# Fewer plain tiles between the staged part and the pair tiles of a feed-forward block, with the operand sums begun a stage earlier

## The chip, the cores and the metric

The kernel runs on one core of a Trainium2 chip. Its inputs are in device memory, and everything that the reference computes, from the modulation vectors to the final norm, is done in one launch. The metric is the device time of one execution in microseconds, as the median of several runs; smaller is better. All arithmetic stands for 32-bit floats: a product is made as three matmuls of split operands (see below), so that its error stays near that of float32.

## The reference

One layer over 256 latent tokens `x` and 256 context tokens `ctx` of width 2048. The change concerns the first half of it only, the two feed-forward products with the same weights for both streams:

```python
h  = h  + 0.5 * mod[:, 2] * swiglu(modulate(h,  norm_ffn1[l], mod[:, 0], mod[:, 1]), w_ffn1_in[l], w_ffn1_out[l])
hc = hc + 0.5 * mc[2]     * swiglu(modulate(hc, norm_ffn1[l], mc[0],     mc[1]),     w_ffn1_in[l], w_ffn1_out[l])

def swiglu(h, w_in, w_out):
    gate, up = jnp.split(h @ w_in, 2, axis=-1)
    return (jax.nn.silu(gate) * up) @ w_out
```

`w_ffn1_in` is 2048 x 11264 (5632 gate columns, 5632 up columns), `w_ffn1_out` 5632 x 2048. Latents and context stand side by side as 512 columns: the first 256 (`:T`) are latents, the others (`T:`) context. Behind it come a mixer (gated linear attention and a convolution), a second feed-forward block for the latents, and a norm; the change does not touch them.

## The kernel before, in words

**Three matmuls for one.** Each operand is split into a high part (rounded to the fast 32-bit matmul type) and a low part (the rest). `split` writes hi with a cast on ACT and lo with a subtraction on DVE; a weight half of 128x1024 becomes `whi` and `wlo` in the same way. A product is then hi·whi + lo·whi + hi·wlo, three matmuls on PE. Every one of those rows is recorded at the helper's line L64, so tiles are told apart by name. Weight halves pass through three buffers (`NW = 3`), raw weights through four (`NRAW = 4`).

**The 44 tiles of hidden columns** (f = 0 to 43, 128 gate and 128 up columns each) are made in three ways.

1. *Tiles 0 to 7, staged over K.* The inner dimension of 2048 is 16 slices of 128 (kt), and `STAGES = [1, 1, 1, 1, 2, 2, 4, 4]` runs over them as they become ready. The last stage holds kt 12 to 15: eight half steps of 24 matmuls of 128x512. Its `evac` adds each product to `part` on DVE; every second one also runs Silu on ACT, a product on DVE, a split into hi and lo, and `keep_hid`, which stores the two to memory by two DMAs that POOL issues (L954).
2. *Plain tiles, f = 8, 9, 10* (`NSTD = 3`, loop `for f in range(NFT0, FT)`, `ffn_tile`): four half steps of 24 matmuls of 128x512 each, 96 in all.
3. *Pair tiles, f = 11 to 43* (`pair_tile`, L866): gate and up, and both token streams, are combined so that seven block products take the place of eight. A block product is 24 matmuls of 128x256, so a pair tile has 168. The seven are, in this order, "11", p, s2, "12", s3, q, "22". Some need sums of weight blocks (`make_t1`, `factor`; the up block is added by an accumulating DMA that POOL issues, L184), and p, s2, s3 and q need sums of the operands.

**The sums of the operands** are made once, by `sums_x(j)` for j = 0 to 7 (L828 to L851); in the texts, sum 1 is j = 0 and sum 8 is j = 7. Each is: two adds on POOL at L831 (`xa`, `xb`: hi + lo of slices j and j + 8); two subtractions on DVE into `xm`; a split of `xm` (hi on ACT, lo on DVE), which is what the second product p and the third, s2, read for slice j; `qf` and `xn` on DVE, and the split of `xn` into `s3`. `place_q` splits `qf` later into the places of the context columns.

**What sets the order.** `after_start` (L814) is a step appended after the last stage: it starts the loads of small tables, opens the pool of the pair tiles, loads the vector `sc` for a wide job on DVE (L653) and runs Silu over it on ACT, and puts the eight `sums_x` into the deque `slow`; `set_rate(HK, 4 * NSTD - 3)` says over how many weight steps they are given out. A list scheduler of the framework then places the instructions of each engine in a queue; what is wrapped in `keep` stays in program order. At run time each queue runs strictly in its order, and semaphores make it wait.

Of the kernel before, what the change touches and what calls it, by code (L numbers as in the profile page):

```python
# [34 lines left out]
NMRAW = 4  # L35
NF2 = 4
HB = 3
NSTD = 3
HK = KT // 2
XP2 = 12  # L40

# [74 lines left out]
def layer_kernel(ctx: ExitStack, tc: tile.TileContext, A):  # L116
# [20 lines left out]
    def gt(p="g", dt=F32, shape=(128, 512), n=512):  # L137
        t = gpool.tile([128, 2 * (T + 2)], dt, tag="g", name=nm(p))[:, :n]
        return t if len(shape) == 2 else t.rearrange("p (a t) -> p a t", a=shape[1])

    def pst():
        return pspool.tile([128, 512], F32, tag="ps", name=nm("ps"))
# [27 lines left out]
    def P(fn):  # L170
        steps.append(("p", None, 0, fn))
# [175 lines left out]
    def set_rate(n, total):  # L347
        rate["credit"], rate["r"] = 0.0, n / total
# [9 lines left out]
    def mm3(ps, w, c, x, start, stop, more=False):  # L358
        hi, lo = w[0][:, c : c + 128], w[1][:, c : c + 128]
        PE.matmul(ps, hi, x[0], start=start, stop=False, skip_group_check=more)  # L360
        PE.matmul(ps, hi, x[1], start=False, stop=False, skip_group_check=more)
        PE.matmul(ps, lo, x[0], start=False, stop=stop, skip_group_check=more)
# [120 lines left out]
    def open_x():  # L483
        modscope.close()
        xbox["t"] = xscope.enter_context(tc.tile_pool(name="xpool", bufs=1))
# [15 lines left out]
    def mod_cols(k0, nk):  # L501
        F = 128 * nk
        g = 1024 // F
        st = {}

        def part(c, u):
            def f(raw):
                if c == 0 and u == 0:
                    st["ps"] = pst()
                for i in range(g):  # L510
                    kt = u * g + i
                    j = kt % 4
                    PE.matmul(
                        st["ps"][32 * j : 32 * j + 32, :F],
                        csil[c][:, kt, :],
                        raw[:, i * F : (i + 1) * F],
                        start=c == 0 and kt < 4,
                        stop=c == 1 and kt >= KT - 4,
                    )
                if c == 1 and kt == KT - 1:  # L520
                    st["msb"] = gt("msb")
                    S.copy(out=st["msb"][:, :F], in_=st["ps"][:, :F])

            return f

        mvs = []
        for c in range(2):
            for u in range(KT // g):
                n = mod_unit[0]
                src = A["wmodK"][n // 2, :, 1024 * (n % 2) : 1024 * (n % 2) + 1024]  # L530
                mvs.append(lambda src=src, fn=part(c, u): M(src, fn))
                mod_unit[0] += 1

        def fin():
            psT = pst()
            for i in range(nk):
                PE.matmul(
                    psT[:, 4 * i : 4 * i + 4], st["msb"][:, i * 128 : (i + 1) * 128], sel, start=True, stop=True
                )
            pv = psT[:, : 4 * nk].rearrange("p (k c v) -> p c k v", c=2, v=2)  # L540
            ks = slice(k0, k0 + nk)
            for v, m, a in ((0, modL, A1L), (1, modC, A1C)):
                V.tensor_tensor(out=m[:, 0:2, ks], in0=pv[:, :, :, v], in1=bmod[:, 0:2, ks], op=ALU.add)
                coef_scale(a[:, ks], m[:, 1, ks], norm(0)[:, ks])

        return mvs, fin
# [104 lines left out]
    def wide_vec(t):  # L651
        xbox["sc"] = t
        nc.sync.dma_start(out=t, in_=A["cvec"][0:1, :].broadcast_to([128, 2048]))  # L653
        keep(S.activation(t, t, AF.Silu))
# [54 lines left out]
    def gate_silu(psg, n=512):  # L709
        p = gt("p")  # L710
        S.activation(p[:, :n], psg, AF.Silu)
        return p
# [9 lines left out]
    NM0 = 2 * NFT0  # L722
# [3 lines left out]
    def prep(si):  # L726
        def f():
            for kt in range(starts[si], starts[si] + STAGES[si]):
                if kt % 2 == 0 and kt:
                    xnorm(kt // 2)  # L730
                xprep1(kt)

        return f

    P(stats1)
    P(norm1a)
    mvs, fin = mod_cols(0, STAGES[0])
# [8 lines left out]
    for si, nk in enumerate(STAGES):  # L746
        kbase = starts[si]
        last = si == len(STAGES) - 1
        per = 16 // nk

        def mstep(un, mm, si=si, nk=nk, kbase=kbase, per=per, last=last):
            m = un * per + mm

            def mm_one(whalf, ps, i, c):
                kt = kbase + i
                mm3(ps, whalf, c, (xh[kt], xl[kt]), i == 0, i == nk - 1)

            def evac(ps):
                if si == 0:
                    part[m] = gt("part")  # L760
                    S.copy(out=part[m], in_=ps)
                else:
                    V.tensor_tensor(out=part[m], in0=ps, in1=part[m], op=ALU.add)
                if last and m % 2 == 1:
                    p = gate_silu(part[m - 1])
                    return finish_keep(m // 2, p, part[m])

            return mm_one, evac

        halfsteps = []  # L770
        for u in range(NM0 // per):
            ms = [mstep(u, mm) for mm in range(per)]

            def half(hf, ms=ms, nk=nk, per=per):
                def f(hi, lo):
                    lates = []
                    for mm in range(per):
                        if mm * nk // 8 != hf:
                            continue
                        ps = pst()  # L780
                        for i in range(nk):
                            ms[mm][0]((hi, lo), ps, i, (mm * nk + i) % 8 * 128)
                        late = ms[mm][1](ps)
                        if late:
                            lates.append(late)

                    def go():
                        for x in lates:
                            x()

                    return go

                return f

            un = Unit(A["w1a"][w0], 2048)
            w0 += 1
            halfsteps += [("w", un, 0, half(0)), ("w", un, 1, half(1))]
        nh = len(halfsteps)
        before, after = [[] for _ in range(nh)], [[] for _ in range(nh)]
        if not last:  # L800
            k1 = kbase + nk
            at = max(0, nh - FINAT)
            mvs, fin = mod_cols(k1, STAGES[si + 1])
            for i, mv in enumerate(mvs):
                before[i * (at + 1) // len(mvs)].append(mv)
            after[at].append(lambda fin=fin, si=si: (P(fin), P(prep(si + 1))))
        for i in range(nh):
            for x in before[i]:
                x()
            steps.append(halfsteps[i])  # L810
            for x in after[i]:
                x()

    def after_start():  # L814
        nc.sync.dma_start(out=smx, in_=A["smallm"])
        nc.sync.dma_start(out=ctri, in_=A["ctri"])
        open_x()
        wide_vec(xbox["t"].tile([128, 2048], F32, name="sc"))
        slow.extend(lambda j=j: sums_x(j) for j in range(HK))
        set_rate(HK, 4 * NSTD - 3)  # L820

    P(after_start)

# [111 lines left out]
    def ffn_tile(wg, wu, f, get_x, fin, n, gate=None):  # L937
        box = {}

        def g(ps):  # L940
            box["p"] = gate(ps) if gate else gate_silu(ps, n)

        in_steps(wg, get_x, g, n)
        in_steps(wu, get_x, lambda ps: fin(f, box.pop("p"), ps, n), n)
# [22 lines left out]
    def finish_keep(f, p, psu, n=512):  # L967
        late = finish_ft(f, p, psu, n)

        def go():  # L970
            late()
            keep_hid(f)
            if f // CH_FT < NCH - 1:
                del hid[f]

        return go
# [58 lines left out]
    for f in range(NFT0, FT):  # L1035
        w = [A["w1b"][2 * (f - NFT0) + i] for i in range(2)]
        if f < NFT0 + NSTD:
            ffn_tile(*w, f, get1, finish_keep, 512)
        else:
            if f == NFT0 + NSTD:  # L1040
                P(flush_slow)
# [992 lines left out]
```

## Time and profile before

| what | value |
|---|---|
| median of the runs | 2707.22 us (2707.12 to 2707.38) |
| the profiled execution's own time | 2703.02 us |
| its span on the core | 2701.3 us |
| PE busy | 2654.8 us, 98% of the span, 18964 matmuls |
| DVE busy | 1878.8 us, 70% |
| ACT busy | 1123.8 us, 42% |
| POOL busy | 188.2 us, 7% |
| mean granted PE clock | 0.995 |
| first matmul of the last stage | 200.69 us |
| first matmul of the first pair tile | 312.15 us |

The shares are of the whole span. What decides about one stage is read in that stage: how many matmuls it has, how long PE stood still in it, and which engine it waited for. A timeline row gives start, duration, engine, line, operation, output tile and input tiles, the count of equal instructions that are put together, and in brackets the idle time of the engine before it with what ended it.

### The profile page before, as it was taken

The page shows a single profiled execution, that of the slowest core. Times are in us where ns is not written, and L with a number is a line of the kernel's source. Part 1 is how long each engine was busy: PE and PEld are TensorE (multiplying, and loading weights), DVE is VectorE, ACT ScalarE, POOL GpSimd, SP SyncE. Part 2 cuts the span into 40 slices and gives each one's busy share as a digit, 9 for nine tenths or more (in the row PEclk, how much of TensorE's full clock was granted, in tenths as well). Part 3 has the DMA queues.
Part 4 walks back from the last instruction along what each step waited for, and adds up shares of the span by engine and source line. Part 5 has one row for each costly group of instructions (what it writes and reads, how often), then busy time and mean ns, then how long its engine had stood idle before and what let it go on. Part 6 is the DMA issues. An engine that isn't in the chain of part 4 may idle for free.

```text
span 2701.3 us, 45665 instructions
## 1 busy us (share of the span) xinstructions
PE 2654.8 (98%) x18964; PEld 2450.7 (91%) x18964; DVE 1878.8 (70%) x2553; ACT 1123.8 (42%) x1498; POOL 188.2 (7%) x212
## 2 busy tenths in 40 slices
PE   7999999999999999999999999999999999999998
PEld 5668899999999988888888988789999999999998
DVE  6656877777777764798799988476876654454543
ACT  5234455554555531122114544254554444444443
POOL 0002311111111100001002100000100000000000
PEclk9999999999999999999999999999999999999999
DMA  9854578778788899669974534455567765555553
GB/s 373 299 183 156 146 221 256 227 235 256 220 256 228 242 326 402 238 233 368 329 247 164 172 123 157 156 184 206 174 223 276 276 228 183 186 182 188 186 186 117
DMA packets 126635, 608.33 MB, mean 225 GB/s; under 512 B 14682, under 2 KB 15066, under 8 KB 78172
## 3 DMA queue, kind: packets, MB, share of 16 engines
q1 hardware_dynamic: 109308, 546.69, 56.7%
q0 software_dynamic: 16544, 57.68, 9.8%
q8 instruction: 148, 2.42, 0.3%
q10 hardware_dynamic: 576, 1.05, 0.1%
q14 instruction: 59, 0.48, 0.0%
HBM read 580.20 MB, written 25.17 MB: 224 GB/s over the span
## 4 chain that ended last, share of the span: by engine, by line
PE 57%; issue 28%; DVE 2%; DMA 0%; ACT 0%; POOL 0%; POOLq 0%; ACTq 0%; DVEq 0%
PE ps L64 57%; DVE wlo L64 1%; DMA raw<-in_w1b 0%; DVE y L64 0%; DVE junk L64 0%; ACT whi L64 0%; DVE E L64 0%; DVE h L64 0%; DVE lo L64 0%; POOL h L1905 0%; DVE raw L64 0%; DVE xs L64 0%; POOLq L2029 0%; ACT L64 0%; DVE t L64 0%
## 5 line engine op out<-in xcount | busy, mean ns | idle before, releaser
L64 PE MATMUL ps<-hi,whi 128*128 128x256 f32 (+1 forms) x4736 | 1441.9, 307 | 9.9 <-ACT whi L64 3.9
L64 PE MATMUL ps<-lo,whi 128*128 128x256 f32 (+1 forms) x4736 | 1446.9, 306 | 0.6 <-DVE lo L64 0.6
L64 PE MATMUL ps<-hi,wlo 128*128 128x256 f32 (+1 forms) x4736 | 1438.4, 306 | 3.4 <-DVE wlo L64 3.3
L64 DVE TENSOR_TENSOR wlo<-raw,whi 128x1024 fp32r<-128x1024 f32 (+1 forms) x654 | 804.1, 1230 | 564.1 <-ACT whi L64 556.0
L64 ACT CAST whi<-raw 128x1024 fp32r<-128x1024 f32 (+1 forms) x654 | 680.1, 1040 | 1235.9 <-PE ps L64 1192.0
L64 PEld LDWEIGHTS ps<-hi,whi 128*128 128x128 f32 x4736 | 892.8, 189 | 67.4 <-issue 11.3
L64 PEld LDWEIGHTS ps<-lo,whi 128*128 128x128 f32 x4736 | 893.4, 189 | 48.5 <-issue 2.9
L64 PEld LDWEIGHTS ps<-hi,wlo 128*128 128x128 f32 x4736 | 891.1, 189 | 49.4 <-DVE wlo L64 4.0
L64 DVE CUSTOM_DVE_ANT_0 junk<-mraw,mraw 128x1024 bf16<-128x1024 f32 x192 | 238.8, 1244 | 4.9 <-DMA mraw<-in_wmodT 1.9
L64 PE MATMUL ps<-hh,wlo 128*128 128x256 f32 x704 | 198.0, 281 | 0.0
L64 PE MATMUL ps<-hh,whi 128*128 128x256 f32 x704 | 197.7, 281 | 0.0
L64 PE MATMUL ps<-hl,whi 128*128 128x256 f32 x704 | 197.4, 280 | 0.0
L64 ACT CAST whi<-t 128x1024 fp32r<-128x1024 f32 x99 | 104.0, 1050 | 148.4 <-PE ps L64 147.8
L64 DVE TENSOR_TENSOR wlo<-t,whi 128x1024 fp32r<-128x1024 f32 x99 | 121.1, 1223 | 40.2 <-ACT whi L64 40.2
L64 PEld LDWEIGHTS ps<-hl,whi 128*128 128x128 f32 x704 | 132.6, 188 | 0.0
L64 PEld LDWEIGHTS ps<-hh,whi 128*128 128x128 f32 x704 | 132.6, 188 | 0.0
L64 PEld LDWEIGHTS ps<-hh,wlo 128*128 128x128 f32 x704 | 132.5, 188 | 0.0
L64 DVE TENSOR_TENSOR part<-ps,part 128x512 f32<-128x512 f32 x112 | 72.6, 685 | 64.8 <-PE ps L64 64.5
L64 PE MATMUL ps<-s,whi 128*128 128x256 f32 x528 | 94.6, 280 | 0.0
L64 PEld LDWEIGHTS ps<-s,whi 128*128 128x128 f32 x528 | 80.5, 188 | 0.0
L64 DVE TENSOR_TENSOR t<-t,raw 128x1024 f32<-128x1024 f32 x66 | 80.4, 1219 | 0.0
L1032 POOL TENSOR_TENSOR nacc<-nacc,sq 128x512 f32<-128x512 f32 x19 | 37.3, 1979 | 572.5 <-ACT sq L64 572.3
(206 smaller groups left out, 2005.2 us busy)
## 6 DMA issues: line engine op xcount, KB each, us to landing
raw<-in_w2b SPq DMA_DIRECT2D x84, 1024.0 KB, 4.9
raw<-in_w1b SPq DMA_DIRECT2D x72, 1024.0 KB, 8.0
raw<-in_wmodT SPq DMA_DIRECT2D x64, 1024.0 KB, 6.3
mraw<-in_wmodT SPq DMA_DIRECT2D x96, 512.0 KB, 5.8
raw<-in_w1o SPq DMA_DIRECT2D x47, 1024.0 KB, 7.4
mraw<-in_wmodK SPq DMA_DIRECT2D x64, 512.0 KB, 7.6
raw<-in_w2o SPq DMA_DIRECT2D x32, 1024.0 KB, 4.9
hi<-hidd SPq DMA_DIRECT2D x80, 256.0 KB, 6.5
```

Of the source, the lines that this page charges most:

```text
L64: i = f(*a, **k)
L1032: eng.tensor_tensor(out=acc, in0=acc, in1=sq, op=ALU.add)
```

## The change

`NSTD` goes from 3 to 1: only f = 8 is a plain tile, and f = 9 to 43 are pair tiles. The body of `after_start` moves into `begin_x`, and the step that calls it is appended before the half steps of the last stage instead of after the staged part. `set_rate` gives the eight sums out over 8 + 4·1 − 2 = 10 weight steps, counted from there; it was 4·3 − 3 = 9, counted from the first plain tile.

```diff
-NSTD = 3
+NSTD = 1
...
+    def after_start():
+        begin_x()
+
...
             halfsteps += [("w", un, 0, half(0)), ("w", un, 1, half(1))]
+        if last:
+            P(after_start)
         nh = len(halfsteps)
...
-    def after_start():
+    def begin_x():
         nc.sync.dma_start(out=smx, in_=A["smallm"])
         nc.sync.dma_start(out=ctri, in_=A["ctri"])
         open_x()
         wide_vec(xbox["t"].tile([128, 2048], F32, name="sc"))
         slow.extend(lambda j=j: sums_x(j) for j in range(HK))
-        set_rate(HK, 4 * NSTD - 3)
-
-    P(after_start)
+        set_rate(HK, NM0 // 2 + 4 * NSTD - 2)
```

Lines behind the change stand three lower in the changed kernel: the adds L831 are L834 there, the stores L954 are L957.

How the queues stand before and now is shown at two places of the program, the start of the last stage and the first pair tile, at the second on three engines. A name ends in a number of its own in each kernel, and the same number in before and now does not mean the same tile.

*ACT at the start of the last stage.* whi373 is a half weight of the stage, hi363 the high part of slice 13, sc the wide vector. Before:

```order
L64 ACTIVATE xs362_1687<-h15_112,modL_79,coef_81 128x256
L64 ACTIVATE xs362_1687<-h16_114,modC_80,coef_81 128x256
L64 CAST whi373_1738<-raw324_1431 128x1024
L64 CAST hi363_1690<-xs362_1687 128x512
L64 ACTIVATE xs365_1696<-h17_116,modL_79,coef_81 128x256
```

Now:

```order
L64 ACTIVATE xs362_1687<-h15_112,modL_79,coef_81 128x256
L64 ACTIVATE xs362_1687<-h16_114,modC_80,coef_81 128x256
L64 CAST whi373_1738<-raw324_1431 128x1024
L64 ACT_TABLE_LOAD
L64 ACTIVATE sc_1748<-sc_1748 128x2048
L64 CAST hi363_1690<-xs362_1687 128x512
L64 ACTIVATE xs365_1696<-h17_116,modL_79,coef_81 128x256
```

A table load and the Silu of sc now stand ahead of hi363; before, the table load stood some rows further on, ahead of the first Silu of p, and the Silu of sc behind the stage.

*ACT around the first pair tile.* In before whi545 is the half weight of the first pair's first product and whi554 that of p; hi522, hi534 and hi550 are the high parts of sums 6, 7 and 8 (hi550 stands three rows below the last row shown, whi554 two below that). Before:

```order
L64 CAST hi522_2424<-xm521_2419 128x512
L64 CAST hi527_2462<-p503_2360 128x512
L64 CAST s3511_2377<-xn524_2429 128x256
L64 CAST whi541_2514<-raw454_2132 128x1024
L64 CAST hi534_2477<-xm533_2472 128x512
L64 CAST s3536_2481<-xn539_2485 128x256
L64 CAST whi545_2546<-raw470_2212 128x1024
L64 ACTIVATE p544_2544<-ps540_2489 128x512
L64 CAST hi62_274<-qf465_2177 128x256
L64 CAST hi96_394<-qf465_2177 128x256
L64 CAST hi135_550<-qf490_2280 128x256
L64 CAST hi166_696<-qf490_2280 128x256
```

Now, where whi520 is the half weight of p, whi531 that of block "12", hi476, hi494 and hi504 the high parts of sums 5, 6 and 7, and p465 and p484 are Silu rows of tiles of the last stage:

```order
L64 CAST whi520_2333<-t1442_2016 128x1024
L64 CAST s3433_1973<-xn453_2041 128x256
L64 CAST hi459_2080<-p456_2073 128x512
L64 ACTIVATE p465_2116<-part107_426 128x512
L64 CAST hi469_2126<-p465_2116 128x512
L64 CAST whi531_2420<-raw408_1893 128x1024
L64 CAST hi476_2141<-xm475_2136 128x512
L64 ACTIVATE p484_2181<-part111_438 128x512
L64 CAST hi201_853<-qf480_2147 128x256
L64 CAST s3478_2145<-xn481_2149 128x256
L64 CAST hi487_2188<-p484_2181 128x512
L64 CAST hi494_2203<-xm493_2198 128x512
```

In before the casts of sums 6 and 7 stand ahead of the first product's half weight and sum 8's ahead of p's; now those of sums 5 to 8 stand behind the half weights of p and of block "12", whi531, whose buffer is that of the first product's.

*POOL around the first pair tile*, from the second half of the sums on. xa and xb are the two adds of a sum, hidd the stores of hid, the rows at L184 accumulating DMAs. Before (sums 5 to 8):

```order
L831 TENSOR_TENSOR xa506_2366<-hi201_853,lo202_854 128x512
L831 TENSOR_TENSOR xb507_2367<-hi360_1683,lo361_1684 128x512
L184 DMA raw496_2318<-in_w1b 128x1024
L831 TENSOR_TENSOR xa519_2417<-hi204_860,lo205_861 128x512
L831 TENSOR_TENSOR xb520_2418<-hi363_1690,lo364_1691 128x512
L954 DMA hidd529_2466<-hi527_2462 128x512
L831 TENSOR_TENSOR xa531_2470<-hi248_1083,lo249_1084 128x512
L831 TENSOR_TENSOR xb532_2471<-hi366_1699,lo367_1700 128x512
L954 DMA hidd530_2467<-lo528_2463 128x512
L831 TENSOR_TENSOR xa547_2550<-hi251_1090,lo252_1091 128x512
L831 TENSOR_TENSOR xb548_2551<-hi369_1706,lo370_1707 128x512
```

Now (sums 5 to 8):

```order
L957 DMA hidd471_2130<-hi469_2126 128x512
L834 TENSOR_TENSOR xa473_2134<-hi201_853,lo202_854 128x512
L834 TENSOR_TENSOR xb474_2135<-hi360_1683,lo361_1684 128x512
L957 DMA hidd472_2131<-lo470_2127 128x512
L957 DMA hidd489_2192<-hi487_2188 128x512
L834 TENSOR_TENSOR xa491_2196<-hi204_860,lo205_861 128x512
L834 TENSOR_TENSOR xb492_2197<-hi363_1690,lo364_1691 128x512
L957 DMA hidd490_2193<-lo488_2189 128x512
L834 TENSOR_TENSOR xa501_2243<-hi248_1083,lo249_1084 128x512
L834 TENSOR_TENSOR xb502_2244<-hi366_1699,lo367_1700 128x512
L834 TENSOR_TENSOR xa513_2292<-hi251_1090,lo252_1091 128x512
L834 TENSOR_TENSOR xb514_2293<-hi369_1706,lo370_1707 128x512
```

Before, the sixteen stores of the last stage all stood ahead of the first add; now they stand between the adds, so that sum 6's adds stand behind a store that waits for ACT's cast hi487, and those of sums 7 and 8 behind one that waits for DVE's lo488.

*PE in the second product of the first pair*, at its slices 4 to 6 before, 5 and 6 now. ps570 is p in before, ps536 now; ps543 is block "12". Before:

```order
L64 MATMUL ps570_2688<-hi500_2327,wlo555_2592 128x256
L64 MATMUL ps570_2688<-hi509_2373,whi554_2591 128x256
L64 MATMUL ps570_2688<-lo510_2374,whi554_2591 128x256
L64 MATMUL ps570_2688<-hi509_2373,wlo555_2592 128x256
L64 MATMUL ps570_2688<-hi522_2424,whi554_2591 128x256
L64 MATMUL ps570_2688<-lo523_2425,whi554_2591 128x256
```

Now:

```order
L64 MATMUL ps543_2495<-hi369_1706,whi531_2420 128x256
L64 MATMUL ps543_2495<-lo370_1707,whi531_2420 128x256
L64 MATMUL ps543_2495<-hi369_1706,wlo532_2421 128x256
L64 MATMUL ps536_2430<-hi476_2141,whi520_2333 128x256
L64 MATMUL ps536_2430<-lo477_2142,whi520_2333 128x256
L64 MATMUL ps536_2430<-hi476_2141,wlo521_2334 128x256
L64 MATMUL ps536_2430<-hi494_2203,whi520_2333 128x256
```

The 24 matmuls of block "12", of which the last three are shown, now stand inside p, between its fourth and fifth slice; before, p's 24 stood in a row.

## Rows read from the trace of the kernel before

**Rows 1.** Utilisation by windows: length, busy time per engine, clock, DMA share, GB/s.

```profile
200.00:300.00 100.00, 99.93 (x432) 80.83 (x431) 75.69 (x92) 42.37 (x59) 29.96 (x35) 1.00 0.46 148
400.00:500.00 100.00, 100.00 (x847) 100.00 (x847) 78.16 (x86) 51.81 (x71) 15.62 (x21) 1.00 0.81 237
```

**Rows 2.** PE's timeline, last stage and first pair; idle before in brackets.

```profile
200.69 1.08 PE L64 MATMUL ps<-hi,whi 128*128 128x512 f32 x4
...
204.40 1.09 PE L64 MATMUL ps<-hi,whi 128*128 128x512 f32 x4
...
312.15 0.28 PE L64 MATMUL ps<-hi,whi 128*128 128x256 f32 x1
...
315.42 0.38 PE L64 MATMUL ps<-hi,whi 128*128 128x256 f32 x1 [0.27 <-ACT whi L64]
...
316.88 0.39 PE L64 MATMUL ps<-hi,wlo 128*128 128x256 f32 x1 [0.96 <-DVE wlo L64]
...
322.33 0.39 PE L64 MATMUL ps<-hi,whi 128*128 128x256 f32 x1 [2.58 <-ACT whi L64]
```

**Rows 3.** Utilisation by windows, last stage and plain tiles.

```profile
210.00:250.00 40.00, 39.93 (x173) 32.05 (x172) 29.45 (x40) 20.50 (x26) 8.81 (x16) 1.00 0.58 203
250.00:310.00 60.00, 60.00 (x261) 48.80 (x260) 49.41 (x55) 19.82 (x29) 24.43 (x22) 1.00 0.42 125
```

**Rows 4.** POOL's timeline in the plain tiles.

```profile
250.06 1.31 POOL L831 TENSOR_TENSOR xa<-hi,lo 128x512 f32<-128x512 f32 x1
...
276.39 1.62 POOL L831 TENSOR_TENSOR xa<-hi,lo 128x512 f32<-128x512 f32 x1
...
280.13 1.61 POOL L831 TENSOR_TENSOR xb<-hi,lo 128x512 f32<-128x512 f32 x1
...
302.06 0.59 POOL L954 DMA_DIRECT2D hidd<-lo  x1 [1.91 <-DVE s L64]
302.67 1.30 POOL L831 TENSOR_TENSOR xa<-hi,lo 128x512 f32<-128x512 f32 x1
```

**Rows 5.** DVE's timeline, plain tiles and first pair.

```profile
257.77 1.22 DVE L64 TENSOR_TENSOR wlo<-raw,whi 128x1024 fp32r<-128x1024 f32 x1 [1.59 <-ACT whi L64]
258.92 0.42 DVE L64 TENSOR_TENSOR xm<-xa,xb 128x256 f32<-128x256 f32 x1
...
275.90 6.40 DVE L64 TENSOR_TENSOR lo<-xm,hi 128x512 fp32r<-128x512 f32 x1 [0.21 <-ACT hi L64]
...
288.46 0.68 DVE L64 TENSOR_TENSOR lo<-xm,hi 128x512 fp32r<-128x512 f32 x1
...
302.47 3.84 DVE L64 TENSOR_TENSOR wlo<-raw,whi 128x1024 fp32r<-128x1024 f32 x1
...
325.09 2.28 DVE L64 CUSTOM_DVE_ANT_0 raw<-raw,sc 128x2048 f32<-128x2048 f32 x1
```

**Rows 6.** ACT's timeline, last stage and plain tiles.

```profile
201.62 0.62 ACT L64 CAST hi<-xs 128x512 fp32r<-128x512 f32 x1
...
215.66 1.28 ACT L64 ACT_TABLE_LOAD   x1
...
247.84 1.91 ACT L64 ACTIVATE sc<-sc 128x2048 f32<-128x2048 f32 x1
...
301.39 1.04 ACT L64 CAST whi<-raw 128x1024 fp32r<-128x1024 f32 x1
```

**Rows 7.** The load of sc: its issue on SP's queue, and all its landings.

```profile
188.73 0.33 SPq L653 DMA_DIRECT2D sc<-in_cvec  x1
...
DMA to landing us min/median/max: 6.1/6.1/6.1
```

**Rows 8.** Utilisation by windows, first pair and a later wait.

```profile
320.00:325.00 5.00, 2.67 (x22) 2.67 (x23) 4.55 (x4) 3.76 (x6) 1.45 (x2) 1.00 0.61 146
1470.00:1475.00 5.00, 1.93 (x15) 1.52 (x13) 5.00 (x9) 3.00 (x7) 2.18 (x1) 1.00 0.56 206
1475.00:1480.00 5.00, 5.00 (x30) 5.00 (x31) 4.32 (x5) 2.94 (x5) 2.89 (x2) 0.66 0.01 3
```

## The prediction

> **What bounds the kernel now.** I read the utilisation by windows first. From 200 to 300 us PE is busy all the time with 432 matmuls of 128x512, so one costs 100 / 432 = 0.2315 us; from 400 to 500, where the pair tiles run evenly, 847 of 128x256 fill the window, 0.118 us each [rows 1]. PE is the bound in both, at full granted clock, so a tile costs its count of matmuls, plus whatever PE waits. Next comes PE's own timeline where the change acts [rows 2]: the last stage begins at 200.69, the three plain tiles follow it without a gap, and the first pair tile begins at 312.15. There PE waits three times, 0.27 + 0.96 + 2.58 = 3.81 us, for whi and wlo, which ACT and DVE make. Third, DVE's share: 29.45 of 40 us in the last stage and 49.41 of 60 in the plain tiles [rows 3]; it has room, but no more than about a fifth in the second stretch. Fourth, the timelines of POOL and DVE [rows 4, 5]: the sixteen adds of the eight sums start at 250.06, the last two at 302.67 and 1.25 later, spread over the plain tiles, and while POOL adds, a DVE subtraction with two SBUF inputs stretches: lo<-xm, 0.68 us when free, takes 6.40 beside the four adds that begin at 276.39, and wlo, 1.22 when free, takes 3.84 at 302.47 although POOL's add is recorded 0.20 later. POOL wins, and DVE finishes when POOL stops.
>
> **Part 1, fewer plain tiles.** A plain tile is 96 matmuls, 96 x 0.2315 = 22.2 us; a pair tile is 168, 168 x 0.118 = 19.8. Two tiles change kind: 2 x (19.83 - 22.22) = **-4.8 us**. These are matmuls of the engine that bounds, so all of it is on the path.
>
> **Part 2, the wide vector's Silu comes earlier.** The order has the table load and ACT's Silu of sc ahead of the cast hi363 of the last stage, instead of behind the stage. The two take 1.28 and 1.91 us [rows 6]. In before hi363 starts at 201.62 and lasts 0.62; it would be ready at 201.6 + 3.2 + 0.6 = 205.45. PE reads it first at 204.40 [rows 2], and in the new order two matmuls stand before it that stood behind, so at 204.86: a wait of **+0.6 us**, with 0 and 1.1 as its ends. Its data are no cause: the load is issued at 188.73 and lands 6.1 later [rows 7]. The table load is the one that stood ahead of p's first Silu at 215.66, so none is added.
>
> **Part 3, the sums move into the last stage, but not all of them.** Before, the adds of sums 1 to 8 have 62 us from 250 to the first pair. Now the first add cannot be issued before the last stage has begun, in POOL's queue the adds stand between the stores of hid, each of which waits for an ACT cast or a DVE subtraction, and the order shows that only sums 1 to 4 stand ahead of ACT's cast for the first pair's second product. Sums 5 to 8 stand behind whi531, the cast that can only start when PE has finished the first product of the pair (its buffer is that of whi511). So they start when PE is already in the pair, and p, the second product, needs all eight: PE's order keeps four of its eight steps, then puts the 24 matmuls of block 12 in between, and then sums 5 to 8 one after the other.
>
> I walk this chain from t0, the end of the first product, about 270.9 (last stage to 245.8, one plain tile of 22.2 to 268.0, 24 matmuls of 0.118 to 270.9). Durations: ACT 1.05 for 128x1024 and 0.62 for 128x512, DVE 1.22, 0.68 and 0.42, a POOL add 1.25 from start to start, a store 0.6 [rows 4 to 6]. (a) whi531 0.1 to 1.15, while POOL has just taken sum 5's two adds (2.5 us) and holds DVE until 2.1: wlo532 3.3. (b) two short xm rows 4.05, hi476 4.75, ACT's Silu 5.3, DVE's lo, qf and xn rows and the product p by 6.85, hi487 7.5. (c) its store 8.2, then sum 6's two adds to 10.7; lo488 stands beside them and ends at 11.3, the store that waits for it at 12.1. (d) now sums 7 and 8 follow without a pause, four adds, 5.0 us, to 17.1: DVE's lo495 is held as in the 6.40 row and ends at 17.7. (e) five short DVE rows to 19.5, hi504 20.2, lo505 21.0, qf and xn 21.7, ACT's Silu of the plain tile and its product 22.3, t2's sum 23.5, the small rows and sum 8's xm to 24.9, ACT's whi523 and copy to 25.6, hi516 26.2, lo517 27.0. PE ends p at 27.2. Without waits the 48 matmuls of p and block 12 would end at 48 x 0.118 = 5.7. PE therefore waits 27.2 - 5.7 = **+21.5 us**. The 3.81 us of waits before [rows 2] are of the same buffers and are inside the walk, so they fall away: **-3.8**.
>
> If POOL's adds held DVE nowhere, (a), (c), (d) and the rest shrink and p would end at about 21.6, a wait of 15.9: that is the lower end. The upper end is a chain in which ACT's and DVE's rows also wait for each other once more at each sum, 4 x 1 us: 25.5.
>
> **Part 4, what follows.** DVE comes out of the chain late, and in the third and fourth product PE waits again for wlo541, which stands behind DVE's wide job of 2.28 us [rows 5], and for the copy of the first product, 0.3: **+2.6**, between 0 and 4. After a wait of PE of 2.50 + 0.56 us, in which it was busy 1.93 of 5, the granted clock of the next 5 us was 0.66 [rows 8], which is (1 - 0.66) x 5 = 1.7 us lost; after the present 2.58 it was not touched. The new waits are longer: **+1.7**, between 0 and 3. From the second pair on, ACT and DVE have their usual order, and the rest of the program differs by single places: 0.
>
> **Sum.** -4.8 - 3.8 + 0.6 + 21.5 + 2.6 + 1.7 = +17.8 us. Against the profiled execution's 2703.0 that is 2720.8; its median of the runs is 4.2 higher, 2707.2, so 2725.0.
>
> The Trainium skill, "SBUF — State Buffer", section "Who interferes with whom", says that VectorE and GpSimd exclude each other by a lock on a shared port, and whoever issued first keeps it. The rows of the 6.40 and 3.84 us agree that they exclude each other, but in the second POOL's recorded start is the later one; nothing in the sum hangs on who issued first.
>
> **Rivals.** (1) *The sums do get done in the last stage.* For it: PE keeps its 45 us there, and DVE is idle a quarter of it. Against it: the order holds half of the sums behind whi531, and all of their 16 adds would have to fit between the stores. It decides at sum 8's lo being ready by 270.9 + 5.4. Then only -4.8 - 3.8 + 0.6 = -8.0 is left: 2699. Chance 0.04. (2) *The chain is there, but DVE is not held by the adds in it.* It decides at lo495 taking 0.7 and not 5. 15.9 in place of 21.5: +12.2, 2719.4. Against it are the two stretched rows above. Chance 0.2. (3) *The waits only eat the gain:* p's wait is 5 to 10 us because sums 5 and 6 are done before t0, DVE being ahead of my walk: between 0 and +5, 2707 to 2712. Against it: hi476 stands behind whi531 on ACT, whatever DVE does. Chance 0.07. (4) *The second pair waits too,* because the sums' late tail shifts the loads and DVE's half-weights: one more wait as long as half the first, 8 to 11: +27, 2734 and more. For it: DVE needs 78.16 of 100 us in even pairs [rows 1], so a backlog of 5 us takes over 20 us to clear; against it: ps2, s3 and q are needed once, and the raw buffers are loaded long before. Chance 0.13. My forecast, slower by 17.8, is on the slower side, and rival (1) is the one on the other.
>
> **How the numbers follow.** Forecast 0.56, rivals 0.04, 0.2, 0.07 and 0.13. The range takes the forecast with the ends of its terms (15.9 to 25.5 for the wait, 0 to 4 for the tail, 0 to 3 for the clock) without all of them at one end at once, 2714 to 2733; that also covers rival (2) and leaves out (1), (3) and most of (4), about 0.2. A measurement of this kernel tells about 0.2%, 5.4 us, from no change: faster 0.04, within 0.07, slower 0.89.
>
> **What would show it.** In the changed kernel's trace: 24 matmuls of 128x256 from about 268, then a run of p and block 12 with PE idle for some 20 us, its releasers DVE lo and ACT hi of xm; POOL adds of sums 5 to 8 within and not before the first pair; a DVE lo of over 4 us beside four adds; whi531's start at the end of the first product; a wait of about 0.6 near 205 for hi. The forecast is wrong if the adds of sum 8 are over by 270, if PE's idle time in the first pair is under 12 us, or if a second gap of over 5 us stands in the second pair.

## The result and the profile after

The changed kernel takes 2721.47 us (four runs, 2717.51 to 2725.38) against 2707.17 for the kernel before: a ratio of 1.0056, interval 1.0043 to 1.0069. It is slower by 14.3 us; 17.8 were forecast, 2725.0 us in a range of 2714 to 2733. Measured once more beside other kernels it took 2723.55 against 2706.49, ratio 1.0067 (1.0052 to 1.0082), slower by 17.1.

The loss has one place. First PE's timeline of the changed kernel, the answer to [rows 2]: start, duration, instruction, and in brackets the idle time before it and what ended it.

```profile
205.93 1.67 PE L64 MATMUL ps<-hi,whi 128*128 128x512 f32 x6 [0.48 <-ACT hi L64]
...
268.65 0.28 PE L64 MATMUL ps<-hi,whi 128*128 128x256 f32 x1
...
274.30 0.38 PE L64 MATMUL ps<-hi,wlo 128*128 128x256 f32 x1 [0.98 <-DVE wlo L64]
...
288.72 0.58 PE L64 MATMUL ps<-hi,whi 128*128 128x256 f32 x1 [11.20 <-ACT hi L64]
...
292.18 0.58 PE L64 MATMUL ps<-hi,whi 128*128 128x256 f32 x1 [1.93 <-ACT hi L64]
...
297.85 0.58 PE L64 MATMUL ps<-hi,whi 128*128 128x256 f32 x1 [4.15 <-ACT hi L64]
...
298.84 0.58 PE L64 MATMUL ps<-lo,whi 128*128 128x256 f32 x1 [0.41 <-DVE lo L64]
299.22 0.42 PE L64 MATMUL ps<-hi,wlo 128*128 128x256 f32 x1
...
303.27 0.34 PE L64 MATMUL ps<-hi,whi 128*128 128x256 f32 x1
...
305.28 0.38 PE L64 MATMUL ps<-hi,whi 128*128 128x256 f32 x1 [1.07 <-ACT whi L64]
```

The first pair tile begins at 268.65, 43.5 us earlier than before, and PE then stands still for 0.98 + 11.20 + 1.93 + 4.15 + 0.41 = 18.67 us inside p, and for 1.07 behind it. The releasers are the casts of sums 6 to 8 (hi), the subtraction of one of them (lo) and, at 274.30, that of a half weight (wlo). Before, the three waits of this place were 3.81 us [rows 2].

Next the utilisation by windows of the same stretch (columns as in [rows 1]; the third number from the right is the granted PE clock), which answers to [rows 8].

```profile
280.00:290.00 10.00, 1.14 (x3) 0.79 (x3) 7.83 (x6) 1.17 (x3) 7.24 (x7) 0.50 0.13 48
290.00:300.00 10.00, 3.37 (x11) 2.24 (x10) 9.06 (x18) 6.51 (x13) 1.52 (x2) 0.50 0.11 9
300.00:310.00 10.00, 8.93 (x63) 8.72 (x61) 8.27 (x12) 4.41 (x7) 1.45 (x2) 0.83 0.96 313
```

PE does three matmuls in the first ten microseconds and eleven in the next, and the granted clock is 0.50, which is 1.2 GHz. It stays there while sum after sum lets three more matmuls through, and is back at 1.00 in the windows after that.

What PE waits for is read on ACT, POOL and DVE, in order of time (answers to [rows 4 to 6]).

```profile
271.62 1.05 ACT L64 CAST whi<-raw 128x1024 fp32r<-128x1024 f32 x1 [2.30 <-PE ps L64]
...
278.80 0.54 POOL L957 DMA_DIRECT2D hidd<-hi  x1 [5.17 <-ACT hi L64]
279.36 1.28 POOL L834 TENSOR_TENSOR xa<-hi,lo 128x512 f32<-128x512 f32 x1
...
281.88 5.67 DVE L64 TENSOR_TENSOR xm<-xa,xb 128x256 f32<-128x256 f32 x1 [2.76 <-POOL xb L834]
...
282.36 1.27 POOL L834 TENSOR_TENSOR xa<-hi,lo 128x512 f32<-128x512 f32 x1
...
286.01 1.25 POOL L834 TENSOR_TENSOR xb<-hi,lo 128x512 f32<-128x512 f32 x1
...
288.05 0.62 ACT L64 CAST hi<-xm 128x512 fp32r<-128x512 f32 x1 [9.65 <-DVE xm L64]
```

The cast whi531 starts when PE has finished the first product. A store of hid stands ahead of sum 6's adds and waits 5.17 us for its cast. Sum 6's subtraction, 0.42 us when free [rows 5], starts at 281.88, is held while POOL makes the four adds of sums 7 and 8 from 282.36 to 287.26, and ends at 287.55. ACT waits 9.65 us for it, and PE 11.20.

To compare kernels I use one more measure, the **front stretch**: from PE's first matmul of the last stage to ACT's Silu of `pu` in the last pair tile (f = 43). Everything the change touches lies in it, and noise from later stages does not. It runs from 200.69 to 974.58 before, 773.89 us, and from 201.12 to 992.14 after, 791.02: **+17.1 us**. In the second profile of the changed kernel it is 790.85. Each kernel gives it for one execution; of the two kernels that were profiled twice the values agree within 0.2 us, and before has one. Here are its parts by the Silu of `pu` in the first pair and in the last, before and then after:

```profile
337.73 0.38 ACT L64 ACTIVATE pu<-ps 128x256 f32<-128x256 f32 x1
...
974.58 0.38 ACT L64 ACTIVATE pu<-ps 128x256 f32<-128x256 f32 x1
```

```profile
314.94 0.38 ACT L64 ACTIVATE pu<-ps 128x256 f32<-128x256 f32 x1
...
992.14 0.38 ACT L64 ACTIVATE pu<-ps 128x256 f32<-128x256 f32 x1
```

Last stage and plain tiles: 111.46 before, 67.53 after. First pair, from its first matmul to that Silu: 25.58 before, 46.29 after. The other pairs: 32 in 636.85 us, 19.90 each, before; 34 in 677.20, 19.92 each, after. So the plain tiles and the even pairs do what was expected of them, and the first pair alone takes 20.7 us more.

### The profile page after: what moved, and what is told of

The parts are those of the page before. It is cut to its first block, busy times and chain, and to the rows that moved or that the text cites. A ratio compares the mean times of both kernels' runs of the same rounds, so it can differ in the third digit from the quotient of the medians.

```text
span 2715.7 us, 46020 instructions
## 1 busy us (share of the span) xinstructions
PE 2649.9 (98%) x19108; PEld 2452.3 (90%) x19108; DVE 1886.5 (69%) x2571; ACT 1133.7 (42%) x1514; POOL 192.3 (7%) x216
## 4 chain that ended last, share of the span: by engine, by line
PE 57%; issue 28%; DVE 3%; ACT 0%; DMA 0%; POOL 0%; POOLq 0%; ACTq 0%; DVEq 0%
PE ps L64 57%; DVE wlo L64 1%; DMA raw<-in_w1b 0%; DVE y L64 0%; DVE xs L64 0%; DVE junk L64 0%; DVE xm L64 0%; ACT whi L64 0%; DVE E L64 0%; DVE h L64 0%; DVE lo L64 0%; ACT hi L64 0%; POOL h L1908 0%; POOLq L2032 0%; ACT L64 0%
## 5 line engine op out<-in xcount | busy, mean ns | idle before, releaser
L64 ACT CAST whi<-t 128x1024 fp32r<-128x1024 f32 x105 | 110.3, 1050 | 156.5 <-PE ps L64 155.2
L64 DVE TENSOR_TENSOR wlo<-t,whi 128x1024 fp32r<-128x1024 f32 x105 | 128.4, 1223 | 41.9 <-ACT whi L64 41.9
L64 PE MATMUL ps<-s,whi 128*128 128x256 f32 x560 | 101.2, 281 | 0.0
L64 PEld LDWEIGHTS ps<-s,whi 128*128 128x128 f32 x560 | 86.1, 189 | 0.0
L64 PE MATMUL ps<-s,wlo 128*128 128x256 f32 x280 | 78.7, 281 | 0.0
```

Source lines behind the costliest of these rows:

```text
L64: i = f(*a, **k)
```

## The experiments

My theory was that the sums of the operands come too late for p: in the changed order half of them stand behind the work that needs PE's first product, POOL's adds wait behind stores of hid, and DVE is held while POOL adds. The rivals were that the earlier start itself costs, that a pair tile costs more than it should whatever the sums do, and that one of POOL or DVE is all of it.

**Only the earlier start.** The changed kernel with three plain tiles.

```diff
-NSTD = 1
+NSTD = 3
```

> Only the earlier start: three plain tiles as before, the sums given out from the last stage on over 18 weight steps. My theory (the loss is the wait for sums 5 to 8 in the first pair, because only one plain tile is left to make them in): no long wait, since the order puts sums 1 to 7 ahead of the first pair; the waits of before, 3.8 us, stay or shrink, plus 0.5 for hi363: -2 to +2 us against before. Rival (the earlier start itself costs, by Silu of sc, POOL's adds and DVE's sums inside the last stage): +5 us or more, as waits of PE between 200 and 312.

Measured: 2702.47 us against 2705.45, ratio 0.9988 (0.9979 to 0.9998). The front stretch is 768.13, 5.8 shorter than before; PE's only wait in it is 0.48 for hi363, and the first pair takes 20.97 from its first matmul to its Silu:

```profile
313.40 0.28 PE L64 MATMUL ps<-hi,whi 128*128 128x256 f32 x1
...
334.37 0.38 ACT L64 ACTIVATE pu<-ps 128x256 f32<-128x256 f32 x1
```

Run again at the end of the study (e12) it was 2701.19 against 2705.01, ratio 0.9986 (0.9978 to 0.9995).

> Only the earlier start, three plain tiles, once more, beside the two-tile kernels of this group: -4 to -1 us against before. If two plain tiles are worth 2.3 us more once the waits are gone, they are faster than this one by 1 to 3 us; if a plain tile costs no more than the pair it makes room for, equal.

So the earlier start is the good half of the change: it removes the 3.81 us of waits of before, and nothing in the last stage pays for it but 0.48. The rest of the 5.8 us is 0.8 more in the first pair and 0.05 in each of the 32 pairs behind it, which no run explains.

**Two plain tiles.** The step between.

```diff
-NSTD = 1
+NSTD = 2
```

> Two plain tiles instead of one, earlier start kept, sums over 14 weight steps. My theory: 22 us more for the sums than the changed kernel has; the order leaves only sums 7 and 8 behind the pair's first product, so the first pair waits 4 to 9 us instead of 18.7, one tile is saved (-2.4), 3.8 of old waits go, +0.5 for hi363: -2 to +4 us against before, and 10 to 16 below the changed kernel. Rival (each tile that becomes a pair costs by itself, whatever the sums do): half of the changed kernel's loss, +7.

Measured: 2711.09 against 2705.45, ratio 1.0018 (1.0008 to 1.0027); front stretch 778.87, +5.0. The waits of the first pair are 3.74 + 0.34 + 2.04 + 0.62 + 1.08 = 7.8 us. The waits are in the forecast range but the time is above it: the granted clock fell to 0.51 around them as well, which I had left out. The +5.0 lies between my range and the rival's +7; what decides against the rival is that the 33 even pairs take 19.89 each, as before, so a pair in the place of a plain tile is not dear by itself, and the loss stands in the first pair.

**The stores of hid off POOL's queue.**

```diff
-            nc.gpsimd.dma_start(out=d, in_=t.bitcast(F32))
+            (nc.sync if f < NFT0 else nc.gpsimd).dma_start(out=d, in_=t.bitcast(F32))
```

> The changed kernel with the stores of hid of tiles 0 to 7 issued by SP's queue instead of POOL's; all else equal. POOL's adds then stand one behind the other and wait for no cast. My theory: all sixteen adds are done in the last stage, the order of ACT has sum 5 ahead of whi531, and DVE's rows from wlo532 to the last lo of sum 8, added up without adds beside them, take 14.9 us after the first product, so the first pair waits 14.9 - 5.7 = 9.2 instead of 18.7: +4 us against before (+0 to +8). Rival (the loss is all of the order on ACT and DVE, POOL only stands by): as the changed kernel, +12 to +15. Rival (the stores delay the weight loads on SP's queue): waits on DMAs of raw, +5 and more over the forecast.

Measured: 2716.66 against 2705.45, ratio 1.0036 (1.0023 to 1.0049); front stretch 782.89, +9.0. PE's timeline in its first pair:

```profile
280.19 0.54 PE L64 MATMUL ps<-hi,whi 128*128 128x256 f32 x1 [2.63 <-ACT hi L64]
...
283.59 0.58 PE L64 MATMUL ps<-hi,whi 128*128 128x256 f32 x1 [1.87 <-ACT hi L64]
...
289.26 0.58 PE L64 MATMUL ps<-hi,whi 128*128 128x256 f32 x1 [4.16 <-ACT hi L64]
```

With the 0.75, 0.19 and 0.42 beside them the waits are 10.0, where 9.2 were worked out from DVE's rows; the 11.20 of the changed kernel is gone. The front stretch gained 8.1 us: the first pair 9.3, while the pairs behind it took 1.0 more. The forecast of +4 was too low mainly because between 280 and 290 PE's clock was granted at 0.51, so the matmuls between the waits ran at half speed, and the first pair took 37.0 us, 15.3 above the 25.58 − 3.81 of a pair without waits, of which 11.1 are waits.

And a part of the expectation was wrong: the adds did not all get done in the last stage. The four of sums 7 and 8 run from 269.51 to 279.16, inside the pair that begins at 268.92, and DVE's two short xm rows beside the last two take 1.50 and 1.37 instead of 0.42. POOL's timeline:

```profile
225.10 1.29 POOL L834 TENSOR_TENSOR xa<-hi,lo 128x512 f32<-128x512 f32 x1 [16.61 <-DVE lo L64]
227.26 1.28 POOL L834 TENSOR_TENSOR xb<-hi,lo 128x512 f32<-128x512 f32 x1 [0.87 <-DMA hidd<-hi]
...
276.06 1.70 POOL L834 TENSOR_TENSOR xa<-hi,lo 128x512 f32<-128x512 f32 x1 [3.77 <-DVE s L64]
```

The operands of all sums are there from about 213 on, when DVE ends its last subtraction of the last stage's slices, but the adds wait for the end of a DVE row or of a store that has nothing to do with the operands. What comes free at such a moment is a tile that the add can write into, in the pool that holds all of these tiles. That this is the cause was not tried by itself.

**The adds on DVE.**

```diff
-            G.tensor_tensor(out=t, in0=xh[k].bitcast(F32), in1=xl[k].bitcast(F32), op=ALU.add)
+            V.tensor_tensor(out=t, in0=xh[k].bitcast(F32), in1=xl[k].bitcast(F32), op=ALU.add)
```

> The changed kernel with the sixteen adds of the sums on DVE instead of POOL; nothing excludes DVE then, but DVE has 16 x 0.6 = 9.7 us more work. My theory: DVE's rows after the first product add up to 19.9 us, so the first pair waits 19.9 - 5.7 = 14.2 us, against 18.7 in the changed kernel: +9.6 us against before (+6 to +12). Rival (DVE's own work is the whole of it): 9.7 us more of it makes it +20. Rival (only POOL's adds and stores make the loss): +0.

Measured: 2716.12 against 2705.45, ratio 1.0033 (1.002 to 1.0046); front stretch 785.15, +11.3. PE waits 0.35 + 2.92 + 2.86 + 5.36 + 0.42 = 11.9 in the first pair, against 18.67, although DVE has sixteen rows more (9.7 us at 0.60 each). Neither rival fits. That the time lies in the forecast range is in part luck: the waits are 2.3 us below the 14.2 expected, and the granted clock of 0.50 between 280 and 290, which I had left out, makes up for it. Stores on SP's queue or adds on DVE take off 8.1 and 5.9 of the 17.1 us. Only the second takes the adds out of the pair; what is left there is with DVE and ACT alone, and PE's three waits for hi are again for sums 6 to 8, which stand behind whi531.

**The hid splits out of the last stage.** The changed kernel, but the splits and stores of tiles 0 to 7 go into a list, and one is taken after each pair tile.

```diff
+    held_hid = deque()
...
+        if 0 <= f < NFT0:
+            held_hid.append(go)
+            return None
         return go
...
             pair_tile(f, *w)
+            for _ in range(1):
+                P(lambda: held_hid and held_hid.popleft()())
```

> The changed kernel with one thing moved: the splits of hid of tiles 0 to 7 into hi and lo, and their stores, are not given out in the last stage but one after each pair tile. POOL's adds then wait for no store, and the order has the casts of sums 1 to 6 ahead of the pair's first half weight. My theory (what makes the sums late is the last stage's hid work in the same three queues): the first pair waits 0 to 4 us instead of 18.7, the waits of before (3.8) go, two tiles are saved (-4.6), +0.5 for hi363: -8 to -3 us against before. Rival (one plain tile is too short for DVE in any order): a wait of 9 as with the stores on SP, +4 and more. Rival (the eight p tiles that are kept longer fill the buffers): waits elsewhere, at the adds or in the last stage.

Measured: 2711.14 against 2706.49, ratio 1.0023 (1.0014 to 1.0033); front stretch 782.14, +8.3. A miss, and the profile says where. In the first pair the waits are 0.88 + 1.64 + 1.90 + 0.99 + 0.78 = 6.2, two thirds less. But every pair that takes a split pays for it. ACT's Silu of `pu` in the first three pairs:

```profile
300.09 0.38 ACT L64 ACTIVATE pu<-ps 128x256 f32<-128x256 f32 x1
...
321.21 0.38 ACT L64 ACTIVATE pu<-ps 128x256 f32<-128x256 f32 x1
...
341.97 0.38 ACT L64 ACTIVATE pu<-ps 128x256 f32<-128x256 f32 x1
```

They come 21.1 and 20.8 apart instead of 19.9, and PE shows a wait of 0.55 to 1.02 for whi in each of eight pairs: the 34 pairs behind the first take 683.9 us in all instead of 677.2. Giving the sums out over 7 weight steps instead of 10 changed nothing for the better:

> As the one before, and the sums given out over 7 weight steps instead of 10; the order then has sums 7 and 8 one place earlier. My theory: 0 to 2 us less wait than with 10 steps, -9 to -4 us against before. Rival (DVE falls behind in the last stage, so wlo is late there): waits of PE between 210 and 265, 2 us or more slower than with 10 steps.

Measured: 2714.09 against 2706.49, ratio 1.0036 (1.0022 to 1.005); front stretch 783.46. The order moved, the waits in the first pair only changed places (3.01 at its longest).

**The same splits in the middle of a pair,** ahead of the fifth product, and `place_q` ahead of the sixth.

```diff
         for i in range(7):
+            if i == 4:
+                P(lambda: held_hid and held_hid.popleft()())
+            if i == 5 and f == NFT0 + NSTD:
+                P(place_q)
             steps.append(("w", u, i, part(i)))
...
-                P(place_q)
```

> One plain tile, the splits of hid of tiles 0 to 7 given out one per pair tile as in the kernel of that kind before, but in the middle of the pair (ahead of its fifth product) and not at its end, where they stood together with the pair's own split and each cost a wait of 0.6 for whi; place_q goes from ahead of the first pair to ahead of its sixth product, which is the first to read what it writes. My theory: the 0.6 to 0.8 us in each of eight pairs (6.4 in all) go, the first pair's waits stay at 4 to 6: -5 to 0 us against before. Rival (DVE and ACT have no slack for the split anywhere in a pair): as before, +3 to +6.

Measured: 2707.53 against 2705.01, ratio 1.0009 (1.0 to 1.0018); front stretch 775.13, +1.2. The waits of 0.6 are gone from all eight pairs (the first two Silu of `pu` are 19.88 apart), so there is room for the split within a pair, only not at its end. The first pair's waits stay (6.15 us), and so does a longer wait for hi363, 1.04 here and in the first of the kernels with later splits. The time is a little above the forecast.

**Two plain tiles, stores on SP's queue, sums over 10 steps.**

```diff
-NSTD = 1
+NSTD = 2
...
-        set_rate(HK, NM0 // 2 + 4 * NSTD - 2)
+        set_rate(HK, 10)
...
-            nc.gpsimd.dma_start(out=d, in_=t.bitcast(F32))
+            (nc.sync if f < NFT0 else nc.gpsimd).dma_start(out=d, in_=t.bitcast(F32))
```

> Two plain tiles, stores of hid of tiles 0 to 7 on SP's queue, sums over 10 weight steps. The order has sums 1 to 6 ahead of the pair's first product and 7 and 8 behind the half weight of p. My theory: 22 us more room and no store ahead of an add, so the first pair waits 1 to 5 us; -2.3 for the tile, -3.8 of old waits, +0.5: -4 to 0 us against before. Rival (room does not help as long as sum 8 is behind p's half weight): waits of 7 us as with two plain tiles alone, +5.

Measured: 2703.28 against 2706.49, ratio 0.9995 (0.9985 to 1.0004); front stretch 771.29, −2.6. The waits are 1.67 for wlo and 1.08 for whi, where two plain tiles alone had 7.8. By the time it cannot be told from before.

**The same with the sums over 8 steps, place_q ahead of the sixth product, and the Silu of sc behind the last stage.**

```diff
-        wide_vec(xbox["t"].tile([128, 2048], F32, name="sc"))
...
-        set_rate(HK, 10)
+        set_rate(HK, 8)
...
+    P(lambda: wide_vec(xbox["t"].tile([128, 2048], F32, name="sc")))
...
+            if i == 5 and f == NFT0 + NSTD:
+                P(place_q)
...
-                P(place_q)
```

> Two plain tiles, stores of hid on SP's queue, sums over 8 weight steps, place_q ahead of the first pair's sixth product, and the Silu of sc back behind the last stage. The order has sums 1 to 7 ahead of the first pair and sum 8 ahead of p's half weight. My theory: hi363's wait of 0.48 is gone and the first pair's 2.8 us fall to 0 to 1: 2 to 4 us below two plain tiles with SP stores, -8 to -4 against before. Rival (what is left of the first pair's waits comes from its own half weights): no change, -3.

Measured: **2697.66 against 2705.01, ratio 0.9971 (0.996 to 0.9982)**, faster than both kernels; front stretch 767.57, −6.3. In the whole stretch PE waits once:

```profile
304.09 0.38 PE L64 MATMUL ps<-hi,whi 128*128 128x256 f32 x1 [1.07 <-ACT whi L64]
```

hi363's wait is gone with the Silu of sc, and all eight sums stand ahead of p's half weight in the order. Against the three-tile kernel with the earlier start (768.05 in the same group) the front stretch is only 0.5 shorter: the tile saves 2.3 and hi363 0.5, but the first pair is 1.3 longer and the even pairs 0.03 each. The medians of the two differ by 3.5, their intervals overlap (0.996 to 0.9982 and 0.9978 to 0.9995), so I take them as close to equal and the gain over before as shown. Three things differ from the kernel with ten steps (the steps, place_q and the Silu of sc), so which of them took away its wait of 1.67 for wlo is not shown. What is left, 1.07, is for the pair's own half weight, as the rival had it.

**Two plain tiles with the splits of hid of tiles 4 to 7 in the middle of the first four pairs,** stores on POOL, sums over 8 steps, `place_q` ahead of the sixth product as above.

```diff
-NSTD = 1
+NSTD = 2
...
-        set_rate(HK, NM0 // 2 + 4 * NSTD - 2)
+        set_rate(HK, 8)
...
+            if i == 4:
+                P(lambda: held_hid and held_hid.popleft()())
...
+        if 4 <= f < NFT0:
+            held_hid.append(go)
+            return None
```

> Two plain tiles, sums over 8 weight steps, stores on POOL, the splits of hid of tiles 4 to 7 given out in the middle of the first four pairs, place_q ahead of the first pair's sixth product. The order has all eight sums ahead of p's half weight. My theory: first pair's waits 0 to 1, +0.5 for hi363, nothing in the four pairs: -8 to -3 against before. Rival (the split costs in the middle of a pair too): 4 x 0.8 more.

Measured: 2703.47 against 2705.01, ratio 0.9991 (0.9982 to 1.0); front stretch 772.36, −1.5. The forecast was too good: with all sums ahead of p in the order, the first pair still waits 0.31 + 1.38 + 1.86, now for its own whi and wlo.

**The changed kernel again,** beside e6 to e8.

> The changed kernel itself once more, beside the kernels of this group. Both theories: 2717 to 2726 us, +11 to +16 against before.

Measured: 2723.55 against 2706.49, as given above; its waits in the first pair are 1.01, 11.22, 1.94, 4.15 and 0.42, the same to 0.03 us as in the first profile.

## Why the prediction was right, step by step

- **Fewer plain tiles, −4.8.** Right. From the last stage to the first pair 43.9 us are gone, with 0.48 of a new wait in it, so a plain tile was 22.2; the even pairs were 19.92 instead of 19.83 in the rows used, two of them 39.84: −4.6.
- **hi363, +0.6.** Measured 0.48 in the changed kernel, 0.48 or 1.04 in every kernel that keeps the Silu of sc there, and gone where it is moved back.
- **The wait in p, +21.5.** The mechanism is as walked, its size 18.67. The end of the first product was put at 270.9 and was about 271.5; p was to end 27.2 behind it and ended 27.9 behind (its last matmul starts at 299.22). The pieces: sum 6's adds start 7.9 behind it (8.2 in the walk); the four adds of sums 7 and 8 end at 15.8 (17.1), because lo488 was not held by sum 6's adds but ran before them. What they held was not lo495 but the first of the two short xm rows of sum 6, by 5.25 us (5.0), so that the second xm row, hi494 and lo495 still stood behind the adds, where the walk had only the end of lo495. lo495 ended 17.9 behind the first product (17.7): two errors of over one us cancel, and that part of the agreement is luck. The wait is smaller than 21.5 though p ended later than walked: of the 27.9 us, 18.7 are waits and 9.2 are the 48 matmuls of p and block "12", which the walk had at 5.7. Part of what I had called wait was slow matmuls.
- **The waits of before, −3.8.** Right, and a little small: the first pair without waits took 20.97 in the kernel with the earlier start and three plain tiles, against 25.58, so the waits of before cost 4.6.
- **What follows, +2.6.** Too high, and not for the reason given. There is one wait of 1.07, not for wlo541 but for a whi, and ACT begins that cast at 304.18, when PE has ended the product before (ACT was idle 2.14 for it). The same 1.07 stands at the same place in the two-tile kernel where no sum is late (e10), so it does not follow from the chain; with three plain tiles it is not there. PE waits nowhere else in the first two pairs.
- **The clock, +1.7.** Right behind p, and too low for the pair; it is the step with the poorest ground, a single later wait [rows 8]. From 280 to 303 the granted clock was 0.50. The nineteen matmuls from 299.22 to 303.27 took 0.213 us each instead of 0.118: 1.8 us, all but the first of them behind p, beside what the slow ones within p took. Over the whole first pair, 46.29 us less the 20.97 of a pair without waits less 18.67 + 1.07 of waits leaves 5.6 us for matmuls that were slow or starting again. What [rows 8] could not tell is that the clock stayed low while PE did three matmuls at a time.
- **The sum.** +17.8 forecast for the profiled execution; the front stretch shows +17.1. The three terms of the first pair, 21.5 + 2.6 + 1.7 = 25.8, stand against 22.2 up to the end of p (27.9 − 5.7), 1.07 and 1.8, together 25.1. The span shows +14.4, since the stages behind the last pair, which the change does not touch, took 3.2 us less in this execution than in the one of before; in the second profile 1.4 less.
- **The rivals.** (1) fell: sums 5 to 8 are in the pair. (2), DVE not held in the chain, would have given +12.2; DVE was held 5.25 us by four adds, so the case is the forecast's, and with the adds on DVE, where nothing holds it, 5.9 us were gone in spite of its sixteen rows more. (3) fell with hi476 behind whi531. (4) fell: the second and later pairs take 19.9.

## What to carry to other kernels

When work that a stage needs is moved earlier and the stage is moved earlier too, compare the room that is left with the work that has to fit into it, and look in the order at which side of the first waiting instruction each piece stands: here half of the sums stood on the wrong side of one cast. An edit of two parts should be tried as two: the earlier start alone was faster, while both as written were slower. Two plain tiles were better than before (0.9971) only with the stores off POOL's queue, the sums earlier in the order and the Silu of sc moved back; with the stores moved and ten steps alone they could not be told from before. Waits that broke a run of matmuls into threes cost twice here, once as waiting and once as half clock.

## What the runs showed of the hardware

Two things I had not expected.

The granted clock stayed at 0.50, 1.2 GHz, from 280 on, through three waits of 11.20, 1.93 and 4.15 us with three matmuls between one and the next, and rose at 303 to 304, after PE had run without a break from 298.84. A similar amount of waiting need not cost the clock: in before the three waits of 0.27, 0.96 and 2.58 us left it at 1.00 in each five microseconds from 312 to 332, while in the last two-tile kernel (e11) three of 0.31, 1.38 and 1.86 went with 0.79 from 295 to 300 and 0.87 from 300 to 305.

Who is held when a DVE row with two SBUF inputs meets a POOL add is not fixed in these runs. The prediction said that POOL wins; in the first pair it did, in both profiles of the changed kernel. But in the mixer stage, near 1490 us, two executions of the changed kernel differ. The first profile's rows, then the second's (e5), POOL's, DVE's and PE's by time:

```profile
1489.00 3.54 POOL L1035 TENSOR_TENSOR nacc<-nacc,sq 128x512 f32<-128x512 f32 x1 [15.93 <-ACT sq L64]
...
1490.11 0.68 DVE L64 TENSOR_TENSOR lo<-xs,hi 128x512 fp32r<-128x512 f32 x1
...
1490.85 0.39 PE L64 MATMUL ps<-lo,whi 128*128 128x256 f32 x1 [0.31 <-DVE lo L64]
```

```profile
1491.26 3.39 POOL L1035 TENSOR_TENSOR nacc<-nacc,sq 128x512 f32<-128x512 f32 x2 [17.46 <-ACT sq L64]
...
1493.45 1.75 DVE L64 TENSOR_TENSOR lo<-xs,hi 128x512 fp32r<-128x512 f32 x1
...
1495.25 0.58 PE L64 MATMUL ps<-lo,whi 128*128 128x256 f32 x1 [2.46 <-DVE lo L64]
```

In the first execution DVE keeps its 0.68 and one POOL add takes 3.54; in the second two POOL adds take 3.39 together and DVE's rows are stretched to 1.75. PE then waits 0.31 for lo in the first and 2.46 in the second. The Trainium skill, "SBUF — State Buffer", section "Who interferes with whom", says that a DVE instruction with two SBUF inputs and a GpSimd instruction that reads SBUF exclude each other, and that whoever issued first keeps the lock; the first half agrees with these rows and with the 5.67 us above, and in the pair the held DVE row was recorded 0.48 us ahead of POOL's add, so who issued first cannot be read from the recorded starts. Such a difference of some 2 us between executions of one program is of the size of what several of the experiments were to tell apart, which is why the front stretch, and not the time alone, is used above.
